# Hybrid decoder layer on Trainium2: the sums of the down stages, of the FFN-up stages and of one operand, moved from GpSimd to VectorE

## Chip, cores, metric

The kernel runs on one core of one Trainium2 chip. The metric is the device time in microseconds of one execution; smaller is better. The times shown are the median of several runs. The profile is one execution recorded by the hardware profiler.

The engines are named in the profile as PE (TensorE, matmuls), PEld (TensorE's weight loads), DVE (VectorE), ACT (ScalarE), POOL (GpSimd) and SP (SyncE, which issues all the transfers here). Each takes its instructions in order.

## The reference, cut to what matters

One layer of a hybrid decoder. After a mixing part (a gated linear recurrence and a gated real recurrence side by side), which the change does not touch, comes a SwiGLU feed-forward network, and a final norm:

```python
# SEQ = 2048 tokens, D_MODEL = 1024, D_FF = 2816, all float32
    h = h + jnp.einsum('bse,ed->bsd', mixed, w_out[l])
    hn = rms_norm(h, ffn_norm_w[l])
    gate, up = jnp.split(jnp.einsum('bsd,df->bsf', hn, w_gate_up[l]), 2, axis=-1)
    h = h + jnp.einsum('bsf,fd->bsd', jax.nn.silu(gate) * up, w_down[l])
return rms_norm(h, final_norm_w)
```

## The kernel before, in words

The 2048 tokens are worked in two halves of 1024 (half 0 and half 1), and a half in two column blocks of 512 tokens. In time the order is: projections and recurrences of half 0, of half 1, FFN-up of half 0, the down stage of half 0, FFN-up of half 1, the down stage of half 1 with the final norm and the stores of the output.

Every float32 operand of a matmul is split in two (`split`): ScalarE rounds it to a high part, VectorE subtracts that from the original and gets the low part. A product is three matmuls: high by high, high by low, low by high. A matmul here has a 128x128 stationary and a 128x512 moving operand.

The FFN's matrix products go by a scheme of Strassen's kind (in Winograd's form): of two by two blocks, seven products `p1` to `p7` are formed from sums and differences of blocks, instead of eight, and the four result blocks are sums of products. So beside the splits there are sums ahead of the products (of weights and of activations) and after them.

- `acts` makes the activation operands of FFN-up, from tiles b11, b12, b21, b22 that are read back from DRAM into `xin` and other tiles. `two` forms the differences; one of them (b12) is on GpSimd.
- `ffn_up` runs over 11 pairs of 256 columns of the FFN width per half, and for each over m = 0 (gate) and m = 1 (up): a "quad" of seven products (L582, tiles `quad_a`, `quad_e`, `quad_f`, `quad_g` in PSUM). The next quad's weights (`Sums.make`, tiles `wgu_a` to `wgu_g`) are made one product at a time between the products of the present one. After each product come a copy or sums out of PSUM (`e1`, `e5`, `u2`, `u3`), SiLU, and the multiplication of gate and up.
- `store` writes the result of a pair to DRAM. For most pairs it first forms four sums of the result blocks (s1 to s4, in `xin` tiles named `as`), which are the activation operands of the down stage; for the last three pairs of half 0 it stores the blocks as they are.
- `down_quads` is the down stage: result blocks h00, h01, h10, h11 (`hd` tiles in SBUF, loaded with the residual) of four token tiles each. The pairs are worked in groups of four: (0..3), (4..7) in half 0 and (0..3), (4..7), (8..10) in half 1. Within a group the products come in the order p1, p2, p6, p5, p3, p7, p4 (`DORDER`; the tiles have letters: p1 a, p2 b, p6 f, p5 e, p3 c, p7 g, p4 d). A product has, for each of four token tiles, 3 matmuls for each pair of the group, at L834: 48 in a group of four, 36 in the group of three. p1 and p2 add up in the same PSUM bank, so do p5 and p3, and p7 and p4.
- `Group.load` fetches the four down-weight blocks (`wdax`, `wdbx`, `wday`, `wdby`), `Group.fetch` the stored activations into raw tiles (`ra_`), and `Group.make` forms the operands of one product, a quarter (one pair of the group) at a time: the splits of the weights (`wd_`) and of the activations (`aop_`), and for p1 and p6 the differences of the weight blocks, of which three are on GpSimd and one (`wdt`) on VectorE. The loop calls it after each token tile's matmuls, for the next product.
- After each token tile of a product its PSUM bank is read. Two partial sums (`e1` = p1 + p6 and `e5` = p5 + p7, in SBUF) are formed with ScalarE copies and VectorE adds, and GpSimd adds them to the result blocks; p2, p3 and p4 are added to them by VectorE.
- In half 0 the last three pairs go through `down_plain` (L721 to L723), an ordinary product, while `acts` runs for half 1 beside it.
- `finish` does the final norm of a token tile and stores it; it is called inside the last group of half 1.

`tt_(out, a, b, op, e)` is an elementwise operation of two operands, on VectorE where no engine is named. Tiles come from pools with a set number of slots: `xin` 4, `late` 5, `block` (128 x 4 x 512) 14, `wslot` 9, `rawt` 3, `page` 16, and 8 banks of PSUM. A tile waits until a slot is free. The order of the instructions on each engine is written by a planner at compile time, which takes them from the program by priority and by times that it assumes (`schedule_with_timeline_sim=True`); it may place work of a later product ahead of an earlier one's. SP issues its transfers in that order too.

Of the kernel before, what the change touches and what calls it, by code (L numbers as in the profile page):

```python
# [13 lines left out]
P = 128  # L14
# [21 lines left out]
def hybrid_layer(ctx: ExitStack, tc: tile.TileContext, x, x_t, norm_w, cols, w_in, gate_w, w_out, w_gu, w_down, out):  # L36
# [453 lines left out]
    def acts(src, nm, direct):  # L490
        ops = {}
        held = []

        def put(name, k, p):
            split([ops[name][s][:, k, :] for s in range(2)], p)

        pages = {}

        def load(k):
            if k == 0:  # L500
                for name in ("p1", "p5", "p6", "p7", "p2") + (("p3", "p4") if direct else ()):
                    ops[name] = [block(f"act_{LET[name]}{s}_{nm}") for s in range(2)]
            b11, b12 = (xin(f"{t}{k}_{nm}") for t in ("b11_", "b12_"))
            b21, b22 = ((late if direct else page)(f"{t}{k}_{nm}") for t in ("b21_", "b22_"))
            for p, n, c in ((b11, 0, 0), (b12, 0, 1), (b22, 1, 1), (b21, 1, 0)):
                nc.sync.dma_start(out=p, in_=src[n][k, :, c * CW : (c + 1) * CW])
            pages[k] = b11, b12, b21, b22

        def one(k):
            b11, b12, b21, b22 = pages[k]  # L510
            put("p1", k, b11)
            tt_(b11, b12, b11, SUB_)
            put("p5", k, b11)

        def two(k):
            b11, b12, b21, b22 = pages[k]
            tt_(b11, b22, b11, SUB_)
            tt_(b12, b22, b12, SUB_, nc.gpsimd)
            put("p2", k, b21)
            put("p6", k, b11)  # L520
            tt_(b21, b21, b11, SUB_)
            put("p7", k, b12)
            if direct:
                put("p3", k, b22)
                put("p4", k, b21)
            held.append((b22, b21))

        def rest(i):
            name = ("p3", "p4")[i]
            ops[name] = [block(f"act_{LET[name]}{s}_{nm}") for s in range(2)]  # L530
            for k in range(4):
                put(name, k, held[k][i])

        steps = [lambda: load(0)]
        for k in range(4):
            steps.append(lambda k=k: (one(k), load(k + 1) if k < 3 else None))
            steps.append(lambda k=k: two(k))
        return ops, steps, [] if direct else [lambda: rest(0), lambda: rest(1)]
# [63 lines left out]
    def ffn_up(half, bops, between=()):  # L602
        between = list(between)
        q0 = half * 2 * NPAIR
        for q in range(q0, q0 + 2 * NPAIR):
# [7 lines left out]
            for i, name in enumerate(ORDER):  # L613
                if q == q0 and i not in s.done:
                    s.make(i)
                product(dst[name], s.op.pop(name), bops[name], i < 4)
                if name == "p1":
                    e1 = page("e1" + nm)
                    nc.scalar.copy(out=e1, in_=b1)
                elif name == "p5":  # L620
                    e5 = page("e5" + nm)
                    nc.scalar.copy(out=e5, in_=b3)
                elif name == "p6":
                    u2 = page("u2" + nm)
                    tt_(u2, e1, b2, ADD)
                elif name == "p7":
                    u3 = page("u3" + nm)
                    tt_(u3, u2, b4, ADD)
                    tt_(e5, u3, e5, ADD, nc.gpsimd)
                    if m == 0:  # L630
                        nc.scalar.activation(out=e5, in_=e5, func=AF.Silu)
                        sg22 = e5
                    else:
                        tt_(e5, e5, sg22, MUL, nc.gpsimd)
                        a22 = e5
                elif name == "p2":
                    if m == 0:
                        sg11 = page("sg11" + nm)
                        nc.scalar.activation(out=sg11, in_=b1, func=AF.Silu)
                    else:  # L640
                        tt_(sg11, sg11, b1, MUL)
                        a11 = sg11
                elif name == "p3":
                    tt_(e1, u2, b3, ADD)
                    if m == 0:
                        nc.scalar.activation(out=e1, in_=e1, func=AF.Silu)
                        sg12 = e1
                    else:
                        tt_(e1, e1, sg12, MUL)
                        a21 = e1  # L650
                else:
                    tt_(u2, u2, b4, ADD)
                    if m == 0:
                        nc.scalar.activation(out=u2, in_=u2, func=AF.Silu)
                        sg21 = u2
                    else:
                        tt_(u2, u2, sg21, MUL)
                        store(half, j, a11, u2, a21, a22)
                if nxt is not None and not end:
                    nxt.make(i)  # L660
                    nxt.done.add(i)
                if between:
                    between.pop(0)()
                if nn is not None and i in (0, 4) and quads[q + 2][0] == half:
                    nn.load(i // 4)
# [4 lines left out]
    def store(half, j, a11, a12, a21, a22):  # L670
# [2 lines left out]
                nc.sync.dma_start(out=a_d[half][2 * j + u][c], in_=p)  # L673
            return
        s1, s2, s3, s4 = (xin(f"as{i}_{half}_{j}") for i in range(4))
        g = nc.gpsimd
        tt_(s1, a21, a22, ADD, g)
        tt_(s2, s1, a11, SUB_, g)
        tt_(s3, a11, a21, SUB_, g)
        tt_(s4, a12, s2, SUB_, g)  # L680
        for name, p in (("p1", a11), ("p2", a12), ("p4", a22), ("p5", s1), ("p6", s2), ("p7", s3), ("p3", s4)):
            nc.sync.dma_start(out=ao_d[half][name][j], in_=p)

# [64 lines left out]
    class Group:  # L748
        def __init__(self, half, j0, n):
            self.half, self.j0, self.n, self.nm = half, j0, n, f"{half}_{j0}"  # L750
            self.a, self.w, self.b, self.raws = {}, {}, None, {}

        def load(self):
            wv = w_down[2 * self.j0 : 2 * (self.j0 + self.n)].rearrange("(g u) p (n w) -> u n p g w", u=2, n=2)
# [15 lines left out]
            self.raws[i] = rs  # L770


        def make(self, i, q):
            name = DORDER[i]
            if q >= self.n:
                return
            if q == 0:
                self.w[name] = [block(f"wd_{LET[name]}{s}_{self.nm}") for s in range(2)]
                self.a[name] = []
            if q % 2 == 0:  # L780
                self.a[name].append([wslot(f"aop_{LET[name]}{s}{q}_{self.nm}", (P, 2, CW)) for s in range(2)])
            b = {k: t[:, q, :] for k, t in self.b.items()}
            if name == "p6":
                if q == 0:
                    self.t2 = block(f"wdt_{self.nm}", F32)
                tt_(self.t2[:, q, :], b[1, 1], b[0, 0], SUB_)
            x = {"p1": b[0, 0], "p2": b[1, 0], "p5": b[0, 0], "p3": b[1, 1], "p7": b[0, 1], "p4": b[1, 0]}.get(name)
            if name == "p6":
                x = self.t2[:, q, :]
            split([self.w[name][s][:, q, :] for s in range(2)], x)  # L790
            split([self.a[name][q // 2][s][:, q % 2, :] for s in range(2)], self.raws[i][q // 2][:, q % 2, :])
            if name == "p1":
                tt_(b[0, 0], b[0, 1], b[0, 0], SUB_, nc.gpsimd)
            elif name == "p6":
                tt_(b[1, 0], b[1, 0], self.t2[:, q, :], SUB_, nc.gpsimd)
                tt_(b[0, 1], b[1, 1], b[0, 1], SUB_, nc.gpsimd)

    def down_quads(half, groups, hp, last):
        groups = [Group(half, j0, n) for j0, n in groups]
# [3 lines left out]
            if s < len(seq):  # L803
                seq[s][0].fetch(seq[s][1])

        def make(s, q):
            if s < len(seq):
                seq[s][0].make(seq[s][1], q)

        groups[0].load()  # L810
        fetch(0)
# [3 lines left out]
        for s, (gr, i) in enumerate(seq):  # L815
            name, nm = DORDER[i], gr.nm
            end = gr is groups[-1]
            if name == "p1":
                e1, e5 = {}, {}
            if name in ("p1", "p5"):  # L820
                ma = [bank(f"pda{name[1]}_{tt}_{nm}") for tt in range(TPC)]
            elif name in ("p6", "p7"):
# [4 lines left out]
            for tt in range(TPC):  # L827
# [8 lines left out]
                        )  # L836
                h00, h01 = hp[tt]
                h10, h11 = hp[TPC + tt]
                if name == "p1":
                    e1[tt] = late(f"e1_{tt}_{nm}")  # L840
                    nc.scalar.copy(out=e1[tt], in_=ps)
                elif name == "p2":
                    tt_(h00, h00, ps, ADD)
                elif name == "p6":
                    tt_(e1[tt], e1[tt], ps, ADD)
                    tt_(h01, h01, e1[tt], ADD, nc.gpsimd)
                elif name == "p5":
                    e5[tt] = xin(f"e5_{tt}_{nm}")
                    nc.scalar.copy(out=e5[tt], in_=ps)
                    tt_(h10, h10, e1[tt], ADD, nc.gpsimd)  # L850
                elif name == "p3":
                    tt_(h01, h01, ps, ADD)
                    tt_(h11, h11, e1[tt], ADD, nc.gpsimd)
                    if end and last:
                        finish(half, tt, hp[tt])
                elif name == "p7":
                    tt_(e5[tt], e5[tt], ps, ADD)
                    tt_(h11, h11, e5[tt], ADD, nc.gpsimd)
                else:
                    tt_(h10, h10, ps, ADD)  # L860
                    if end and last:
# [246 lines left out]
```

## Time and profile before

| | us |
|---|---|
| median of 3 runs (lowest, highest) | 2206.64 (2205.87, 2207.19) |
| the profiled execution | 2208.05 |
| its span, first to last instruction | 2206.3 |
| TensorE busy | 2121.9 (96%) |
| VectorE busy | 1508.5 (68%) |
| ScalarE busy | 1019.4 (46%) |
| GpSimd busy | 587.7 (27%) |
| FFN-up of half 0 and half 1 begin, about | 870, 1543 |
| down stage of half 0 and half 1 begin, about | 1295, 1962 |
| `down_plain` begins | 1467 |
| mean granted clock of TensorE | 0.985 |

A row of the page's groups gives line, engine, operation, written tile and read tiles, sizes and count, then busy time in all and mean ns of one, then how long the engine sat idle just before, and what ended most of that. A row of waits gives: engine and line, for whom, us in total, times, the longest. A row of the timeline gives: start, us, engine, line, operation, tiles, count of merged instructions, and in brackets the idle time before. A row of stretches gives: from:to, its length, then busy us and (instructions) of PE, PEld, DVE, ACT and POOL, then the granted clock, the busy share of the transfer engines, and GB/s.

A matmul's recorded time (some 390 ns) overlaps with the next one's, so the pitch, the time of a stretch over its matmuls, says more than the busy time.

### The profile page before, as it was taken

How to read it: one execution, taken by the hardware profiler on the slowest of the kernel's cores; microseconds unless marked ns; L12 is line 12 of the kernel's file. 1: busy time of each engine (PE TensorE's matmuls, PEld its weight loads, DVE VectorE, ACT ScalarE, POOL GpSimd, SP SyncE). 2: the span in 40 equal slices, each digit the busy share in tenths (PEclk: the TensorE clock that was granted, in tenths of full speed). 3: DMA queues.
4: the chain of work that ended last, by engine and by line, in shares of the span. 5: the costliest groups of instructions: out<-in, count | busy, mean ns of one | idle time of the engine just before them, and what ended most of it. 6: DMA issues, size and time to landing. Idle time of an engine off the chain costs nothing. (4 is left out here: it accounts for less than half of the span.)

```text
span 2206.3 us, 27183 instructions
## 1 busy us (share of the span) xinstructions
PE 2121.9 (96%) x9956; PEld 1744.7 (79%) x9956; DVE 1508.5 (68%) x2314; ACT 1019.4 (46%) x1757; POOL 587.7 (27%) x442
## 2 busy tenths in 40 slices
PE   8999899999999999999999998998999999998998
PEld 6778788887777887788888876887788888876876
DVE  5566664635677557866676579777767666679897
ACT  5467664535677545433333343444333333343443
POOL 1111110101111101223232146411323232356455
PEclk9999999999999999999999999999999999999999
DMA  6111105851110056423232264355423232355423
GB/s 220 58 39 39 39 20 169 285 167 30 38 39 29 20 181 230 150 98 106 91 125 91 96 227 164 115 160 169 134 91 124 91 124 91 105 209 196 153 86 139
DMA packets 137414, 261.33 MB, mean 118 GB/s; under 512 B 11072, under 2 KB 27456, under 8 KB 137280
## 3 DMA queue, kind: packets, MB, share of 16 engines
q1 hardware_dynamic: 137280, 259.59, 35.1%
q8 instruction: 78, 1.28, 0.2%
q14 instruction: 56, 0.46, 0.1%
HBM read 196.37 MB, written 63.18 MB: 118 GB/s over the span
## 5 line engine op out<-in xcount | busy, mean ns | idle before, releaser
L484 POOL TENSOR_TENSOR e<-u,e 128x512 f32<-128x512 f32 x44 | 77.3, 1757 | 525.3 <-ACT wgu_c L198 307.0
L484 POOL TENSOR_TENSOR hd<-hd,e 128x512 f32<-128x512 f32 x80 | 121.5, 1550 | 142.4 <-DVE e L484 142.3
L582 PE MATMUL quad_e<-act_e,wgu_e 128*128 128x512 f32 x528 | 129.2, 393 | 2.0 <-ACT wgu_e L198 1.9
L582 PE MATMUL quad_f<-act_f,wgu_f 128*128 128x512 f32 x528 | 127.1, 389 | 1.5 <-ACT wgu_f L198 1.5
L582 PE MATMUL quad_g<-act_d,wgu_d 128*128 128x512 f32 x528 | 127.6, 390 | 0.0
L582 PE MATMUL quad_a<-act_a,wgu_a 128*128 128x512 f32 x528 | 127.3, 389 | 0.0
L582 PE MATMUL quad_g<-act_g,wgu_g 128*128 128x512 f32 x528 | 127.1, 389 | 0.0
L582 PE MATMUL quad_a<-act_b,wgu_b 128*128 128x512 f32 x528 | 127.0, 389 | 0.0
L582 PE MATMUL quad_e<-act_c,wgu_c 128*128 128x512 f32 x528 | 126.8, 389 | 0.0
L582 PEld LDWEIGHTS quad_e<-act_e,wgu_e 128*128 128x128 f32 x528 | 100.1, 190 | 24.0 <-ACT wgu_e L198 2.6
L582 PEld LDWEIGHTS quad_f<-act_f,wgu_f 128*128 128x128 f32 x528 | 99.1, 188 | 22.4 <-ACT wgu_f L198 1.8
L582 PEld LDWEIGHTS quad_a<-act_a,wgu_a 128*128 128x128 f32 x528 | 98.9, 188 | 20.9 <-issue 0.4
L582 PEld LDWEIGHTS quad_a<-act_b,wgu_b 128*128 128x128 f32 x528 | 99.1, 188 | 20.6
L582 PEld LDWEIGHTS quad_e<-act_c,wgu_c 128*128 128x128 f32 x528 | 99.1, 188 | 20.6
L582 PEld LDWEIGHTS quad_g<-act_g,wgu_g 128*128 128x128 f32 x528 | 99.0, 188 | 20.6
L582 PEld LDWEIGHTS quad_g<-act_d,wgu_d 128*128 128x128 f32 x528 | 98.9, 188 | 20.4
L484 DVE TENSOR_TENSOR u<-u,quad_g 128x512 f32<-128x512 f32 x88 | 60.4, 686 | 79.3 <-PE quad_g L582 79.2
L226 PE MATMUL pb<-xn,wlo_in 128*128 128x512 f32 x256 | 102.7, 401 | 0.0
L225 PE MATMUL pb<-xn,whi_in 128*128 128x512 f32 x256 | 102.4, 400 | 0.0
L227 PE MATMUL pb<-xn,whi_in 128*128 128x512 f32 x256 | 101.8, 398 | 0.0
L155 DVE TENSOR_TENSOR wlo_in<-raw_in,whi_in 128x1024 fp32r<-128x1024 f32 x48 | 60.7, 1265 | 60.0 <-PE pv L238 40.6
L226 PE MATMUL pa<-xn,wlo_in 128*128 128x512 f32 x256 | 100.9, 394 | 0.0
(316 smaller groups left out, 5521.2 us busy)
## 6 DMA issues: line engine op xcount, KB each, us to landing
raw<-in_w_gu SPq DMA_DIRECT2D x88, 512.0 KB, 3.8
raw_in<-in_w_in SPq DMA_DIRECT2D x48, 512.0 KB, 3.5
ao_p<-as SPq DMA_DIRECT2D x76, 256.0 KB, 2.3
raw_o<-in_w_out SPq DMA_DIRECT2D x32, 512.0 KB, 4.7
x<-in_x SPq DMA_DIRECT2D x32, 256.0 KB, 5.3
xrh<-in_x SPq DMA_DIRECT2D x32, 256.0 KB, 3.9
h<-h SPq DMA_DIRECT2D x32, 256.0 KB, 3.7
hn<-hths SPq DMA_DIRECT2D x32, 256.0 KB, 4.5
```

The lines of the kernel that those rows point to most:

```text
L155: v.tensor_tensor(out=lo, in0=raw, in1=f(hi), op=ALU.subtract)
L225: nc.tensor.matmul(ps, lhsT=whi[:, ks], rhs=hi, start=(k == 0), stop=False)
L226: nc.tensor.matmul(ps, lhsT=wlo[:, ks], rhs=hi, start=False, stop=False)
L227: nc.tensor.matmul(ps, lhsT=whi[:, ks], rhs=lo, start=False, stop=(k == KT - 1))
L484: (e or v).tensor_tensor(out=out, in0=a, in1=b, op=op)
L582: nc.tensor.matmul(ps, lhsT=w[:, s, ks], rhs=x, start=first and k + n == 0, stop=k == 3 and n == 2, skip_group_check=not first)
```

## The change

- In `acts`, `ffn_up` and `store`, every sum that GpSimd did goes to VectorE.
- In the down stage GpSimd does no sums any more. p5 and p7 are added to h11 straight from PSUM, each by VectorE. p1 + p6 is added up over all the groups in one tile `u2` per token tile (four `xin` tiles, held through the whole down stage; ScalarE copies the first p1 into it), and only after p6 of the last group is it added to h01, h10 and h11.
- `Group.make` works in four parts of another cut: parts 0 and 1 split the weights, two pairs at a time (128x1024), parts 2 and 3 the activations, two pairs at a time. The differences of weight blocks are formed in one instruction over the whole group, on VectorE: `wdt` ahead of p6's part 0, and one after part 1 of each of p1, p6 and p5.

```diff
--- before.py
+++ after.py
@@ -515,7 +515,7 @@
         def two(k):
             b11, b12, b21, b22 = pages[k]
             tt_(b11, b22, b11, SUB_)
-            tt_(b12, b22, b12, SUB_, nc.gpsimd)
+            tt_(b12, b22, b12, SUB_)
             put("p2", k, b21)
             put("p6", k, b11)
             tt_(b21, b21, b11, SUB_)
@@ -626,12 +626,12 @@
                 elif name == "p7":
                     u3 = page("u3" + nm)
                     tt_(u3, u2, b4, ADD)
-                    tt_(e5, u3, e5, ADD, nc.gpsimd)
+                    tt_(e5, u3, e5, ADD)
                     if m == 0:
                         nc.scalar.activation(out=e5, in_=e5, func=AF.Silu)
                         sg22 = e5
                     else:
-                        tt_(e5, e5, sg22, MUL, nc.gpsimd)
+                        tt_(e5, e5, sg22, MUL)
                         a22 = e5
                 elif name == "p2":
                     if m == 0:
@@ -673,11 +673,10 @@
                 nc.sync.dma_start(out=a_d[half][2 * j + u][c], in_=p)
             return
         s1, s2, s3, s4 = (xin(f"as{i}_{half}_{j}") for i in range(4))
-        g = nc.gpsimd
-        tt_(s1, a21, a22, ADD, g)
-        tt_(s2, s1, a11, SUB_, g)
-        tt_(s3, a11, a21, SUB_, g)
-        tt_(s4, a12, s2, SUB_, g)
+        tt_(s1, a21, a22, ADD)
+        tt_(s2, s1, a11, SUB_)
+        tt_(s3, a11, a21, SUB_)
+        tt_(s4, a12, s2, SUB_)
         for name, p in (("p1", a11), ("p2", a12), ("p4", a22), ("p5", s1), ("p6", s2), ("p7", s3), ("p3", s4)):
             nc.sync.dma_start(out=ao_d[half][name][j], in_=p)
 
@@ -748,7 +747,7 @@
     class Group:
         def __init__(self, half, j0, n):
             self.half, self.j0, self.n, self.nm = half, j0, n, f"{half}_{j0}"
-            self.a, self.w, self.b, self.raws = {}, {}, None, {}
+            self.a, self.w, self.b, self.raws, self.t2 = {}, {}, None, {}, None
 
         def load(self):
             wv = w_down[2 * self.j0 : 2 * (self.j0 + self.n)].rearrange("(g u) p (n w) -> u n p g w", u=2, n=2)
@@ -770,30 +769,29 @@
             self.raws[i] = rs
 
 
-        def make(self, i, q):
-            name = DORDER[i]
-            if q >= self.n:
-                return
-            if q == 0:
+        def make(self, i, part):
+            name, n, b = DORDER[i], self.n, self.b
+            if part == 0:
                 self.w[name] = [block(f"wd_{LET[name]}{s}_{self.nm}") for s in range(2)]
-                self.a[name] = []
-            if q % 2 == 0:
-                self.a[name].append([wslot(f"aop_{LET[name]}{s}{q}_{self.nm}", (P, 2, CW)) for s in range(2)])
-            b = {k: t[:, q, :] for k, t in self.b.items()}
-            if name == "p6":
-                if q == 0:
+                self.a[name] = [[wslot(f"aop_{LET[name]}{s}{k}_{self.nm}", (P, 2, CW)) for s in range(2)] for k in range(0, n, 2)]
+                if name == "p6":
                     self.t2 = block(f"wdt_{self.nm}", F32)
-                tt_(self.t2[:, q, :], b[1, 1], b[0, 0], SUB_)
-            x = {"p1": b[0, 0], "p2": b[1, 0], "p5": b[0, 0], "p3": b[1, 1], "p7": b[0, 1], "p4": b[1, 0]}.get(name)
-            if name == "p6":
-                x = self.t2[:, q, :]
-            split([self.w[name][s][:, q, :] for s in range(2)], x)
-            split([self.a[name][q // 2][s][:, q % 2, :] for s in range(2)], self.raws[i][q // 2][:, q % 2, :])
-            if name == "p1":
-                tt_(b[0, 0], b[0, 1], b[0, 0], SUB_, nc.gpsimd)
-            elif name == "p6":
-                tt_(b[1, 0], b[1, 0], self.t2[:, q, :], SUB_, nc.gpsimd)
-                tt_(b[0, 1], b[1, 1], b[0, 1], SUB_, nc.gpsimd)
+                    tt_(self.t2[:, 0:n, :], b[1, 1][:, 0:n, :], b[0, 0][:, 0:n, :], SUB_)
+            k = 2 * (part % 2)
+            m = min(n, k + 2)
+            if part < 2:
+                x = {"p1": b[0, 0], "p2": b[1, 0], "p5": b[0, 0], "p3": b[1, 1], "p7": b[0, 1], "p4": b[1, 0]}.get(name, self.t2)
+                split([self.w[name][s][:, k:m, :] for s in range(2)], x[:, k:m, :])
+            else:
+                split([t[:, 0 : m - k, :] for t in self.a[name][k // 2]], self.raws[i][k // 2][:, 0 : m - k, :])
+            if part == 1:
+                d, x, y = {
+                    "p1": (b[0, 0], b[0, 1], b[0, 0]),
+                    "p6": (b[0, 1], b[1, 1], b[0, 1]),
+                    "p5": (b[1, 0], b[1, 0], self.t2),
+                }.get(name, (None, None, None))
+                if d is not None:
+                    tt_(d[:, 0:n, :], x[:, 0:n, :], y[:, 0:n, :], SUB_)
 
     def down_quads(half, groups, hp, last):
         groups = [Group(half, j0, n) for j0, n in groups]
@@ -803,9 +801,11 @@
             if s < len(seq):
                 seq[s][0].fetch(seq[s][1])
 
-        def make(s, q):
+        def make(s, part):
             if s < len(seq):
-                seq[s][0].make(seq[s][1], q)
+                seq[s][0].make(seq[s][1], part)
+
+        u2 = {}
 
         groups[0].load()
         fetch(0)
@@ -815,8 +815,6 @@
         for s, (gr, i) in enumerate(seq):
             name, nm = DORDER[i], gr.nm
             end = gr is groups[-1]
-            if name == "p1":
-                e1, e5 = {}, {}
             if name in ("p1", "p5"):
                 ma = [bank(f"pda{name[1]}_{tt}_{nm}") for tt in range(TPC)]
             elif name in ("p6", "p7"):
@@ -836,26 +834,28 @@
                         )
                 h00, h01 = hp[tt]
                 h10, h11 = hp[TPC + tt]
+
                 if name == "p1":
-                    e1[tt] = late(f"e1_{tt}_{nm}")
-                    nc.scalar.copy(out=e1[tt], in_=ps)
+                    if tt not in u2:
+                        u2[tt] = xin(f"u2_{tt}_{nm}")
+                        nc.scalar.copy(out=u2[tt], in_=ps)
+                    else:
+                        tt_(u2[tt], u2[tt], ps, ADD)
                 elif name == "p2":
                     tt_(h00, h00, ps, ADD)
                 elif name == "p6":
-                    tt_(e1[tt], e1[tt], ps, ADD)
-                    tt_(h01, h01, e1[tt], ADD, nc.gpsimd)
+                    tt_(u2[tt], u2[tt], ps, ADD)
+                    if end:
+                        for p in (h01, h10, h11):
+                            tt_(p, p, u2[tt], ADD)
                 elif name == "p5":
-                    e5[tt] = xin(f"e5_{tt}_{nm}")
-                    nc.scalar.copy(out=e5[tt], in_=ps)
-                    tt_(h10, h10, e1[tt], ADD, nc.gpsimd)
+                    tt_(h11, h11, ps, ADD)
                 elif name == "p3":
                     tt_(h01, h01, ps, ADD)
-                    tt_(h11, h11, e1[tt], ADD, nc.gpsimd)
                     if end and last:
                         finish(half, tt, hp[tt])
                 elif name == "p7":
-                    tt_(e5[tt], e5[tt], ps, ADD)
-                    tt_(h11, h11, e5[tt], ADD, nc.gpsimd)
+                    tt_(h11, h11, ps, ADD)
                 else:
                     tt_(h10, h10, ps, ADD)
                     if end and last:
```

## The prediction

> **What bounds the kernel now.** I read the page first (busy shares), then the waits of TensorE, then busy time by stretches, and last the instructions of VectorE and GpSimd inside the bad stretches.
>
> ```profile
> span 2206.3 us, 27183 instructions
> PE 2121.9 (96%) x9956; PEld 1744.7 (79%) x9956; DVE 1508.5 (68%) x2314; ACT 1019.4 (46%) x1757; POOL 587.7 (27%) x442
> L484 POOL TENSOR_TENSOR hd<-hd,e 128x512 f32<-128x512 f32 x80 | 121.5, 1550 | 142.4 <-DVE e L484 142.3
> ...
> PE pda L834 <- DVE aop_c L199: 15.7, 4, 7.4
> PE pdb L834 <- DVE wd_f L199: 6.2, 2, 3.2
> PE pd L721 <- ACT act_d L198: 3.6, 1, 3.6
> ```
>
> TensorE is busy nearly throughout, and its longest waits on VectorE lie in the down stages (L834). What they cost is seen in stretches. The first two rows hold the down products' matmuls alone (half 0, half 1), the others all engines: PE, PEld, DVE, ACT and POOL busy us, granted clock, DMA share, GB/s.
>
> ```profile
> 1298.06:1467.20 169.14, 157.80 (x671) 128.44 (x670) 0.96 0.46 151
> 1965.15:2196.40 231.25, 216.27 (x923) 174.98 (x922) 0.97 0.42 144
> ...
> 870.00:1294.00 424.00, 420.11 (x1864) 346.60 (x1865) 284.45 (x392) 162.75 (x290) 106.55 (x69) 1.00 0.33 114
> 1288.00:1346.30 58.30, 55.13 (x237) 45.16 (x236) 53.97 (x59) 29.76 (x57) 36.77 (x24) 0.97 0.75 269
> 1346.30:1369.30 23.00, 14.82 (x50) 10.72 (x49) 23.00 (x19) 5.99 (x11) 18.41 (x11) 0.78 0.31 93
> 1369.30:1467.20 97.90, 97.90 (x434) 81.06 (x433) 68.89 (x94) 36.85 (x65) 37.38 (x25) 1.00 0.39 121
> 1467.20:1541.00 73.80, 69.54 (x294) 56.37 (x293) 60.51 (x90) 38.35 (x73) 9.24 (x8) 0.95 0.53 175
> 1975.80:1994.20 18.40, 14.62 (x55) 10.94 (x53) 18.40 (x18) 9.85 (x20) 12.99 (x8) 0.91 0.36 125
> 2017.10:2038.90 21.80, 14.20 (x50) 10.39 (x50) 21.80 (x18) 5.99 (x11) 18.51 (x11) 0.77 0.30 97
> 2038.90:2127.10 88.20, 87.19 (x386) 71.91 (x384) 77.98 (x91) 37.44 (x68) 46.08 (x28) 1.00 0.39 128
> 2139.10:2196.40 57.30, 57.27 (x253) 47.11 (x251) 45.13 (x65) 25.89 (x57) 26.08 (x21) 1.00 0.34 115
> 2196.40:2206.30 9.90, 0.00 (x0) 0.00 (x0) 5.60 (x11) 2.56 (x8) 1.65 (x3) 0.66 0.57 213
> ```
>
> 1369.3 to 1467.2 holds nine products of 48 matmuls without a wait: 97.90 / 432 = 0.2266 us a matmul. At that pitch the down stages would need 671 x 0.2266 = 152.0 and 923 x 0.2266 = 209.2 us; they take 169.1 and 231.3. So 17.1 + 22.1 = 39.2 us are lost, nearly all in the first group of each half. The worst stretches are 1346.3 and 2017.1: there VectorE is busy for all of it (23.00 of 23.00, 21.80 of 21.80) and GpSimd for 80%. Part of a loss is an after-effect: the granted clock is 0.78 there, and the slowest matmul below takes twice the usual one.
>
> ```profile
> L834 PE MATMUL pda<-wd_c,aop_c x228: 387/389/797, 1346.3 to 2179.7; 128*128 128x512 f32 x114
> ...
> 1356.89 12.54 PE L834 MATMUL pda<-wd_c,aop_c 128*128 128x512 f32 x40 [7.42 <-DVE aop_c L199]
> ...
> 1319.13 2.48 DVE L199 TENSOR_TENSOR wd_c<-wdby,wd_c 128x512 fp32r<-128x512 f32 x4
> 1348.37 6.79 DVE L199 TENSOR_TENSOR wd_a<-wdax,wd_a 128x512 fp32r<-128x512 f32 x4
> 1355.09 3.43 DVE L199 TENSOR_TENSOR aop_c<-ra_c,aop_c 128x512 fp32r<-128x512 f32 x2
> 1367.60 1.87 DVE L484 TENSOR_TENSOR hd<-hd,pda 128x512 f32<-128x512 f32 x3
> ...
> 1351.23 6.74 POOL L484 TENSOR_TENSOR wdax<-wday,wdax 128x512 f32<-128x512 f32 x4
> 1504.55 1.21 DVE L199 TENSOR_TENSOR wlo_d<-raw_d,whi_d 128x1024 fp32r<-128x1024 f32 x1
> 2197.66 1.41 DVE L739 SCALAR_TENSOR_TENSOR hd<-hd,ss_f,wfin 128x512 f32<-128x512 f32 x2
> ```
>
> This is the cause. Four VectorE subtractions of 128x512 take 2.48 us, 0.60 each start to start. The same four take 6.79, 1.70 each, while GpSimd runs its own at 1.69 (6.74 / 4). TensorE waits 7.42 us for aop_c, which stands behind them. An add whose second operand is in PSUM keeps 0.60 (1.87 for three).
>
> **The change, part by part.** The sum is made against the profiled execution: 2208.05 us, 1.75 more than its span; the median shown, 2206.64, is 1.4 lower.
>
> VectorE's load in a down group of four. Before, its own instructions at 0.60: 56 splits, 20 adds and 4 subtractions (wdt), 48 us. GpSimd runs 16 adds of 1.55 and 12 subtractions of 1.69 beside it, 45 us, in which VectorE does 0.60/1.70 of its work: up to 29 us lost. Together 77 us, for 7 x 48 x 0.2266 = 76.1 us of TensorE: saturated. After: 28 splits of 128x1024 at 1.14 (1.21 less the 0.07 by which neighbours overlap), 32 us; 28 adds at 0.60, 17 us; four 128x2048 subtractions. These no row shows: the step from 0.60 to 1.14 for 512 more elements gives an estimate of 2.22, four narrow ones give 2.40; I take 2.2, so 9 us. Sum 58 of 76 us. For the VectorE page of the Trainium skill ("VectorE: DVE Perf Modes", section on the TRN2 errata) a 2048-element f32 tensor_tensor is 2.29 us; an estimate by it is 0.4 us more a group, and no run shows it yet. GpSimd's 45 us go.
>
> Last group of half 1 (three pairs): 14 splits of 1.14 and 14 of 0.60, 28 adds, 4 subtractions of 1.66, 12 adds of the sum u2, eight finishes of 1.35 (1.41 for the two of one): 24 + 17 + 7 + 7 + 11 = 66 us, for 57.1 of TensorE and the tail of 9.9. Tight, but before it held 50 and GpSimd's interference and lost almost nothing (57.30 us at 2139.1 for 252 matmuls, 57.1).
>
> What remains of the 39.2 us:
> (a) In p6 of the last group each token tile gets three more adds: 16 x 0.60 = 9.6, with p5's activations and its wide subtraction (2.3 + 2.2; 1.7 + 1.7 with three pairs) 14.1 us of VectorE against 10.9 of TensorE in half 0, 13.0 against 8.2 in half 1. From 0 (TensorE needs none of the adds, if p5's operands come first) to 3.2 + 4.8 = 8. I take 4.
> (b) u2 takes all four xin tiles for the whole down stage, where e5 took them late. In half 1 these last hold the sums of the last store, and p2, on p1's banks, waits for the copy into u2. ScalarE's queue holds its casts behind that copy.
>
> ```profile
> 1975.20 1.72 POOL L484 TENSOR_TENSOR as<-e,e 128x512 f32<-128x512 f32 x1
> 1987.05 1.74 POOL L484 TENSOR_TENSOR as<-u,as 128x512 f32<-128x512 f32 x1
> ...
> 1965.15 10.82 PE L834 MATMUL pda<-wd_a,aop_a 128*128 128x512 f32 x47
> ...
> ao_p<-as SPq DMA_DIRECT2D x7, 256.0 KB, 3.4
> ```
>
> The four sums end at 1988.8, and stores land 3.4 us after issue, while p1 ends at 1976.0: kept as late, this costs up to 16 us. On VectorE, each 0.60 after its last input, they can be out before. 0 to 16; I take 2, as three of the four need no input later than p3's product.
> (c) The planner's order is unknown: a wide instruction ahead of a needed one delays by 1.1 to 2.2 us, where it was 6.8. Later groups lost 0 (1369.3) and 88.20 - 384 x 0.2266 = 1.2 us: 0 to 10 over five groups, I take 4.
> Down stages: -39.2 + 10 = -29.
>
> Here one rule stands against the merge. "Perfetto Trace Analysis" of the Trainium skill (section on optimizing Scalar/DVE operations) advises breaking up instructions where an unsaturated engine causes bubbles elsewhere; by the rows, a half-width split is ready 0.54 us sooner, and with a wait in each of five groups the sum by it is 2.7 us less gain. No run shows this yet.
>
> Plain stage (L721): 73.80 - 294 x 0.2266 = 7.2 us lost.
>
> ```profile
> 1493.54 3.32 POOL L484 TENSOR_TENSOR b<-b,b 128x512 f32<-128x512 f32 x2 [13.70 <-DVE b L484]
> 1494.10 3.31 DVE L199 TENSOR_TENSOR act_e<-b,act_e 128x512 fp32r<-128x512 f32 x2
> 1503.57 0.76 PE L721 MATMUL pd<-whi_d,ad 128*128 128x512 f32 x1 [3.57 <-ACT act_d L198]
> ```
>
> Moving b12 to VectorE costs 0.60 a piece and frees 2.1 us of act_e's 3.3; on the path to act_d I take -2, between 0 and -7.
>
> FFN-up. 22 + 11 + up to 44 instructions a half go to VectorE, 77 x 0.60 = 46 us, and contention goes:
>
> ```profile
> L484 DVE TENSOR_TENSOR s<-raw,raw 128x512 f32<-128x512 f32 x44 | 45.4, 1032 | 42.3 <-DMA raw<-in_w_gu 42.3
> L484 DVE TENSOR_TENSOR s<-s,raw 128x512 f32<-128x512 f32 x44 | 46.0, 1046 | 1.3
> L484 DVE TENSOR_TENSOR u<-u,u 128x512 f32<-128x512 f32 x22 | 37.0, 1681 | 0.0
> L484 DVE TENSOR_TENSOR s<-raw,s 128x512 f32<-128x512 f32 x44 | 30.4, 691 | 1.6 <-DMA hn<-hths 0.4
> ```
>
> Against the undisturbed 0.69 that is 22 x (0.34 + 0.36) + 11 x 0.99 = 26 us back a half: 284 becomes about 305 of 424 us. TensorE does not wait there; what hides it is VectorE's 140 us of idle time, and if that cover went, the 20 us a half would be the price. I take 0 (-2 to +3). The tail (9.9 us with no matmul) keeps its chain: 0 (-1 to +1).
>
> Sum: -29 - 2 = -31: 2208.05 becomes 2177, and the median 2206.64 - 31 = 2175.6. All gone: -39.2 - 7.2 - 1 - 2, 2157. All ends bad: -39.2 + 34 + 4, about 2205.
>
> **The rivals.**
> Half the gain: VectorE still ends last at the first groups, or is saturated in the last ones; (a) to (c) then cost 20 to 30: 2186 to 2200, say 2191. For it: 66 of 67 us of load in the last group. Against it: 58 of 76 us elsewhere, and GpSimd's 45 us, which cost VectorE up to 29. "Perfetto Trace Analysis" of the Trainium skill, in the section already named, says that offloading to GpSimd may make sense where DVE is saturated, which speaks for this rival; no run shows it yet.
> No change: the first groups wait for transfers, which move no sooner, 2206. For it: DMA share 0.75 from 1288. Against it: 0.31 and 93 GB/s where TensorE stands still.
> Slower: activations late. Parts 0 and 1 now make weights, and the raw tiles come free only at parts 2 and 3, while the next fetch is still asked for at the second token tile, so SP stands there with the next loads behind it.
>
> ```profile
> 1365.30 5.76 SPq L768 DMA_DIRECT2D ra_a<-ao_p  x2
> ...
> ra_a<-ao_p SPq DMA_DIRECT2D x2, 512.0 KB, 3.6
> ```
>
> Now already the second of a pair is issued up to 5.8 us after the first. If it comes half a product (5.4 us) later and lands 3.6 after issue, it may miss the next product's start. Each of 35 products late by 0.9 us cancels the 31; by 2 us, 70 - 31 gives 2246. Against it: activation tiles come free only at a product's end, so the splits were no earlier before.
>
> **How the numbers follow.** Likeliest, most of the loss gone (2157 to 2186): 0.66. Half: 0.18. No change: 0.05. Slower: 0.11. Within 0.2% (4.4 us) counts as the same, about what a measurement here can tell. Half and likeliest are both faster, 0.84. The range 2160 to 2203 leaves out the slower case, no change and a little of the best end.
>
> **What would show it.** GpSimd without f32 128x512 sums in the down stages; wd and aop splits at 1.2 us for twice the width, none at 1.7 per 512; the stretches after p1 and in p3 of the first groups near 0.2266 us a matmul at clock 1.00; FFN-up unchanged in length. Wrong would be: waits of pda or pdb for aop or wd of over 3 us, u2's copy waiting for a store's DMA, casts waiting for ra tiles in steady groups.

## The result, and the profile after

The changed kernel takes 2168.0 us (median; 2166.54 to 2170.55), the kernel before 2206.26 in the same series: 0.9828 of it, 95% interval 0.9811 to 0.9845. That is 38 us less, inside the range given (2160 to 2203), 7.6 below the number 2175.6. Its profiled execution took 2167.16, with a span of 2165.5 where it was 2206.3.

The head of the page, after:

```profile
span 2165.5 us, 26664 instructions
PE 2108.4 (97%) x9956; PEld 1740.6 (80%) x9956; DVE 1483.9 (69%) x2395; ACT 993.8 (46%) x1599; POOL 131.4 (6%) x155
```

The longest of TensorE's waits for an aop or wd tile (total us, times, longest):

```profile
PE pdb L832 <- DVE aop_f L199: 4.4, 1, 4.4
```

GpSimd's busy time went from 588 to 131 us, and VectorE, which took over its sums, is busy 25 us less than before (1483.9 for 1508.5), with 81 instructions more (2395 for 2314). Of the waits for aop and wd tiles one is left.

The stretches after. First the down products' matmuls alone, up to p4's last (half 0, half 1), as the first two rows shown of before:

```profile
1295.42:1447.50 152.08, 152.08 (x671) 125.79 (x670) 1.00 0.49 165
1939.17:2156.10 216.93, 212.53 (x923) 175.07 (x922) 0.98 0.46 155
```

Then all engines (length, then PE, PEld, DVE, ACT and POOL busy with their counts, granted clock, DMA share, GB/s):

```profile
865.00:1292.50 427.50, 423.55 (x1871) 350.03 (x1870) 297.45 (x453) 161.48 (x278) 5.62 (x4) 0.99 0.35 118
1295.40:1447.50 152.10, 152.10 (x672) 125.98 (x671) 126.15 (x142) 60.09 (x68) 0.00 (x0) 1.00 0.49 165
1447.50:1514.00 66.50, 66.07 (x291) 54.19 (x290) 53.60 (x82) 34.55 (x66) 2.84 (x5) 1.00 0.55 182
1949.80:1965.70 15.90, 11.52 (x38) 8.90 (x37) 12.76 (x14) 2.15 (x3) 0.00 (x0) 0.79 0.91 319
2156.10:2165.50 9.40, 0.00 (x0) 0.00 (x0) 4.98 (x9) 2.16 (x8) 1.26 (x3) 0.72 0.49 185
```

Half 0's down stage takes 152.1 us where it took 169.1: nothing above the pitch is left of the 17.1 us lost. Half 1's takes 216.9 where it took 231.3; 923 x 0.2266 = 209.2, so 7.7 of the 22.1 remain. `down_plain` takes 66.5 where the stretch took 73.8. The tail is 9.4 for 9.9.

VectorE's instructions in half 1's down stage, in order of time, after (start, duration):

```profile
1935.08 1.22 DVE L199 TENSOR_TENSOR wd_b<-wdbx,wd_b 128x1024 fp32r<-128x1024 f32 x1
1941.35 2.29 DVE L484 TENSOR_TENSOR wdt<-wdby,wdax 128x2048 f32<-128x2048 f32 x1
1943.55 2.29 DVE L484 TENSOR_TENSOR wday<-wdby,wday 128x2048 f32<-128x2048 f32 x1
```

And the group of one product of FFN-up:

```profile
L484 DVE TENSOR_TENSOR u<-u,u 128x512 f32<-128x512 f32 x22 | 15.1, 686 | 0.0
```

A split of twice the width takes 1.22 us, where the narrow one took 1.70 beside GpSimd; a 128x2048 difference takes 2.29, and 2.20 from start to start. The product u<-u,u of FFN-up, 1.68 us before, takes 0.69.

The 7.7 us of half 1 are nearly all at one place: from 1949.80 to 1965.70, 38 matmuls, 8.6 us at the pitch, take 15.90. TensorE's rows there:

```profile
1939.17 10.82 PE L832 MATMUL pda<-wd_a,aop_a 128*128 128x512 f32 x47
1949.82 1.98 PE L832 MATMUL pdb<-wd_f,aop_f 128*128 128x512 f32 x8
1956.17 9.74 PE L832 MATMUL pdb<-wd_f,aop_f 128*128 128x512 f32 x29 [4.38 <-DVE aop_f L199]
1965.75 2.88 PE L832 MATMUL pda<-wd_b,aop_b 128*128 128x512 f32 x12
```

ScalarE's rows there, with what ended the wait before each:

```profile
1960.57 0.58 ACT L841 COPY u<-pda 128x512 f32<-128x512 f32 x1 [9.20 <-DMA ao_p<-as]
1970.85 1.20 ACT L841 COPY u<-pda 128x512 f32<-128x512 f32 x2 [3.43 <-DMA ao_p<-as]
```

The store's four sums on VectorE:

```profile
1951.42 0.69 DVE L484 TENSOR_TENSOR as<-e,e 128x512 f32<-128x512 f32 x1
...
1959.43 0.70 DVE L484 TENSOR_TENSOR as<-as,sg 128x512 f32<-128x512 f32 x1
1960.03 0.70 DVE L484 TENSOR_TENSOR as<-sg,e 128x512 f32<-128x512 f32 x1
1960.64 0.70 DVE L484 TENSOR_TENSOR as<-u,as 128x512 f32<-128x512 f32 x1
```

p1's bank is free for p2 only when ScalarE has copied it to u2, and u2 stands in xin tiles that the last store's sums (as) still hold: ScalarE waits 9.20 us for their transfer. Two things make the sums and their transfers late. In VectorE's order splits for p5, p6 and p3 stand between the first sum and the second, which starts 8 us after it; and the transfers land 9.5 us after issue (median of the four), where the row of before had 3.4, while the transfer engines are busy for 0.91 of this stretch. In TensorE's order p6 stands ahead of p2 there, and waits 4.38 us for its own activations; the granted clock of the whole stretch is 0.79.

### The profile page after: what moved, and what is told of

Same layout as the page of the kernel before. It is cut to its first block, busy times and chain, and to the rows that moved or that the text cites. A ratio compares the mean times of both kernels' runs of the same rounds, so it can differ in the third digit from the quotient of the medians.

```text
span 2165.5 us, 26664 instructions
## 1 busy us (share of the span) xinstructions
PE 2108.4 (97%) x9956; PEld 1740.6 (80%) x9956; DVE 1483.9 (69%) x2395; ACT 993.8 (46%) x1599; POOL 131.4 (6%) x155
## 4 chain that ended last, share of the span: by engine, by line
PE 78%; ACT 8%; DVE 8%; DMA 2%; issue 2%; POOL 1%; DVEq 0%; SPq 0%; ACTq 0%; POOLq 0%
PE quad_e L582 11%; PE quad_a L582 11%; PE quad_g L582 11%; PE pda L832 9%; PE pdb L832 6%; PE quad_f L582 6%; PE poh L237 2%; PE poh L239 2%; PE poh L238 2%; PE pb L226 1%; PE pb L227 1%; PE pb L225 1%; DMA b<-hn 1%; PE pa L225 1%; PE pa L226 1%
## 5 line engine op out<-in xcount | busy, mean ns | idle before, releaser
L238 PE MATMUL poh<-wlo_o,mx 128*128 128x512 f32 x256 | 99.5, 392 | 1.2 <-DVE wlo_o L155 1.2
L225 PE MATMUL pa<-xn,whi_in 128*128 128x512 f32 x256 | 100.5, 393 | 0.0
```

Of the source, the lines that this page charges most:

```text
L225: nc.tensor.matmul(ps, lhsT=whi[:, ks], rhs=hi, start=(k == 0), stop=False)
L238: nc.tensor.matmul(ps, lhsT=hi, rhs=wlo[:, ks], start=False, stop=False)
```

## The experiments

The theory was the prediction's: GpSimd's sums slow VectorE's two-input instructions, and where VectorE's load then passes TensorE's time, TensorE waits. Rivals: the wide instructions and the carried sum made the gain; the moves in FFN-up made it; TensorE had been waiting for GpSimd's results. Each time is a median beside the kernel before on the same chip; the ratio to it, with its interval, is what is compared.

**Only the engine of the down sums.** The kernel before, and:

```diff
-            tt_(h01, h01, e1[tt], ADD, nc.gpsimd)    # and h10, h11 with e1, h11 with e5
+            tt_(h01, h01, e1[tt], ADD)
-            tt_(b[0, 0], b[0, 1], b[0, 0], SUB_, nc.gpsimd)    # and the two of p6
+            tt_(b[0, 0], b[0, 1], b[0, 0], SUB_)
```

> The kernel before, with only one thing changed: the seven kinds of down-stage sums that GpSimd did (three differences of weight blocks, four adds into h) go to VectorE; no wider instructions, no carried u2, FFN-up and the other operands as before. Theory (GpSimd's two-input sums slow VectorE's two-input sums from 0.60 to 1.70 us per 128x512): VectorE's load in a group of four is 76 x 0.60 + 28 x 0.60 = 62 to 65 us of 76, the 39 us lost in the down stages fall to under 12, time 2170 to 2185. Rival (the gain is of the wider instructions and of the carried sum): the down stages still lose over 25 us, time 2192 or more.

2167.66 us, 0.9825 (0.9808 to 0.9841): as fast as the whole change, and faster than the theory said. Half 1's down products in it:

```profile
1945.60:2154.90 209.30, 209.30 (x923) 173.06 (x922) 1.00 0.47 160
```

No loss at all, and half 0's take 152.09 us (1294.94 to 1447.03), the pitch too. The rival falls: this needs no wide instruction and no carried sum.

**Only the other sums.** The kernel before, with the changes of `acts`, `ffn_up` and `store` alone (their four edits in the diff).

> The kernel before, with only the sums of FFN-up, of the store and of b12 moved to VectorE; down stages as before. Theory: FFN-up had no loss to give back; the plain stage gains up to its 7 us and the start of FFN-up up to 3; the down stages still lose 35 to 42 us: time 2196 to 2204. Rival (the changed kernel's gain comes largely from VectorE being ahead after FFN-up): below 2190.

2194.36 us, 0.9944 (0.9929 to 0.9958): 12 us, between the two expectations. The down stages lose less than they were to:

```profile
1298.00:1464.50 166.50, 156.09 (x671) 125.82 (x671) 0.98 0.45 154
1955.40:2182.50 227.10, 216.21 (x923) 174.87 (x922) 0.98 0.43 146
```

By the pitch 14.5 and 17.9 us, where 35 to 42 together were expected and 39.2 were lost before. Before, GpSimd did the four `as` sums and the last quad's sums inside half 1's first group; that their move to VectorE is the cause was not tried by itself. The plain stage gave back its 7 us here too (65.9 us from its first matmul to FFN-up's):

**Only b12.** The kernel before, and `tt_(b12, b22, b12, SUB_)` without GpSimd.

> The kernel before with only the difference b12 on VectorE. Theory (the plain stage's loss came through GpSimd's b12 and the tiles it held): the plain stage loses under 2 us instead of 7, time 2198 to 2202. Rival (that gain came from VectorE being ahead through the moves in FFN-up): 2204 to 2208.

2201.46 us, 0.9977 (0.9968 to 0.9987), as the theory said. In its trace the plain stage runs from the first row to the last:

```profile
1461.01 0.39 PE L721 MATMUL pd<-whi_d,ad 128*128 128x512 f32 x1
...
1526.88 0.39 PE L723 MATMUL pd<-whi_d,ad 128*128 128x512 f32 x1
```

65.9 us where it was 72.7 (1467.2 to 1539.9). One instruction per step on another engine gives nearly the whole of that term. The time of the traced execution (2196.59, the lowest of ten) says less than the stage: there FFN-up of half 0 began at 863.0, and in the three traces with the same code up to there (up_sums_dve, all_sums_dve, reads_two) at 867.5 to 868.1.

**All sums, nothing else.** The two edits above together, on the kernel before.

> The kernel before, with all its GpSimd sums on VectorE (down stages, FFN-up, store, b12) and nothing else changed: narrow instructions, e1 and e5 as before. Theory (the move of engine is the whole gain, and the new cut with u2 costs its 7.8 us): 2153 to 2162. Rival (wide instructions and the carried sum give a part of the gain): 2166 or more.

2158.98 us, 0.9780 (0.9762 to 0.9799), which is better than the changed kernel (0.9828; the intervals do not meet). Both down stages run at the pitch:

```profile
1296.82:1448.90 152.08, 152.08 (x671) 125.79 (x670) 1.00 0.50 168
1939.88:2149.10 209.22, 209.22 (x923) 173.05 (x922) 1.00 0.48 161
```

So the new cut of `make` and u2 brought nothing here, and lost 7.7 us of what the move had won in half 1.

**u2 elsewhere.** The changed kernel, and:

```diff
-                        u2[tt] = xin(f"u2_{tt}_{nm}")
+                        u2[tt] = (late if half else xin)(f"u2_{tt}_{nm}")
```

> The changed kernel, with u2 of half 1 in tiles of the pool late instead of xin, which the last store's four sums hold. Theory (the 7.8 us that half 1's down stage still loses come from u2's copy waiting for those stores, so that the planner puts p6 ahead of p2): p2 follows p1, no wait for aop_f, 2158 to 2163. Rival (the loss is of VectorE's backlog at the group's start): 2166 to 2171.

2160.12 us, 0.9787 (0.9770 to 0.9805). Half 1:

```profile
1940.61:2149.80 209.19, 209.19 (x923) 173.05 (x922) 1.00 0.48 160
```

TensorE's rows at the place where the changed kernel lost them:

```profile
1940.61 10.82 PE L832 MATMUL pda<-wd_a,aop_a 128*128 128x512 f32 x47
1951.27 11.04 PE L832 MATMUL pda<-wd_b,aop_b 128*128 128x512 f32 x48
1962.14 11.04 PE L832 MATMUL pdb<-wd_f,aop_f 128*128 128x512 f32 x48
```

p2 follows p1 and the 7.7 us are gone. That the tiles of the store held u2 back is shown; the chosen slot, not VectorE's backlog, cost it: in this run too VectorE is busy for all of the 27 us from 1935 to 1962.

**Narrow pieces.** The changed kernel, with each split and difference in pieces of 128x512 (a loop over q around them).

> The changed kernel, with every split and every difference of weight blocks cut back into pieces of 128x512. Theory (VectorE has room: 62 of 76 us in a group of four): TensorE waits no longer than now, 2164 to 2172. By the Trainium skill's advice to break up instructions, operands are ready half a microsecond sooner: 2164 to 2167. Rival (the wide instructions carry the gain): 2175 or more.

2166.12 us, 0.9812 (0.9796 to 0.9828): not to be told from the changed kernel. The advice of "Perfetto Trace Analysis" in the Trainium skill (section on optimizing Scalar/DVE operations) to break up instructions would have given 2.7 us by the prediction's estimate, less than these intervals resolve. One trace has the wait for aop_f at 3.2 instead of 4.4 us.

**GpSimd reads for nothing.** The changed kernel, with `nc.gpsimd.tensor_tensor(out=carry[:, 0], in0=d, in1=d, op=ADD)` per token tile and product, d an idle tile touched by `nc.scalar.copy(out=d[:, 0, 0:4], in_=ps[:, 0:4])`.

> The changed kernel, with one added GpSimd sum of 128x512 per token tile and product in the down stages (28 a group), of a tile that nothing uses into a tile that nothing uses, released by a small ScalarE copy out of the product's bank; no other work depends on it. It computes nothing that the output needs. Theory (shared reading): while it runs VectorE's two-input SBUF instructions slow down to GpSimd's pace (128x1024 from 1.2 to over 2.5 us), the down stages lose 20 to 45 us again: 2188 to 2215. Rival (the old loss came from waiting for GpSimd's results, or from the planner's order): no dependence, so 2164 to 2174.

2195.87 us, 0.9952 (0.9934 to 0.9969): as the theory said, but not for its reason alone. Its trace shows TensorE waiting for the small copies, which wait for GpSimd:

```profile
PE pda L839 <- ACT sct L814: 5.9, 7, 2.1
PE pdb L839 <- ACT sct L814: 4.5, 4, 2.4
PE pd L720 <- ACT sct L814: 2.5, 3, 1.5
```

That is a coupling that the experiment made itself, 13 us of its 28, so it decides nothing.

**GpSimd writes for nothing.** The same copies, with three `nc.gpsimd.memset(d, 0.0)` in place of the sum.

> As the run with the added GpSimd sums, but the added work is three memsets of 128x512 (0.5 us each at the kernel's start), which write and read nothing. Theory (it is the reading of two inputs that meets VectorE's): VectorE's instructions keep 1.2 us per 128x1024, time 2164 to 2174. Rival (any busy GpSimd, or the small ScalarE copies, cost it): like the run with the sums, 2188 or more.

2169.28 us, 0.9828 (0.9809 to 0.9848): no effect. GpSimd is busy 81 us of half 0's 152, as the row of the stretch shows (POOL before the clock):

```profile
1298.00:1450.10 152.10, 152.10 (x672) 125.98 (x671) 125.49 (x143) 66.09 (x122) 81.03 (x160) 1.00 0.49 165
```

VectorE's splits keep their 1.22 (the group; total us, mean ns):

```profile
L199 DVE TENSOR_TENSOR aop_e<-ra_e,aop_e 128x1024 fp32r<-128x1024 f32 x4 | 4.9, 1222 | 0.6 <-PE pda L840 0.4
```

A GpSimd that is busy with memsets costs VectorE nothing; it is not its being busy as such.

**Reads again, released by GpSimd itself.** The sum as before, after `nc.gpsimd.tensor_copy(out=d[:, 0, 0:4], in_=h[:, 0:4])` of a result tile.

> The changed kernel with the added GpSimd sums once more, now released by a small GpSimd copy of four columns of the result tile that VectorE has just written, so that no PSUM bank and no ScalarE instruction waits for them (in the last group's p3 and p4 there are none). It computes nothing that the output needs. Theory (shared reading slows VectorE by itself): two-input splits of 128x1024 again at 1.5 to 1.9 us, 2180 to 2200, with TensorE waiting for aop and wd tiles. Rival (the 28 us of the first such run came from the ScalarE copies that TensorE waited for): 2166 to 2174.

2175.77 us, 0.9851 (0.9829 to 0.9873): between both expectations. Half 0 as one stretch:

```profile
1298.30:1450.50 152.20, 152.20 (x672) 125.93 (x672) 144.89 (x140) 57.66 (x65) 122.39 (x106) 1.00 0.49 163
```

And two of VectorE's groups there, an add from PSUM and a split with both inputs in SBUF:

```profile
L484 DVE TENSOR_TENSOR hd<-hd,pda 128x512 f32<-128x512 f32 x24 | 15.5, 675 | 0.5 <-PE pda L842 0.5
L199 DVE TENSOR_TENSOR wd_e<-wdax,wd_e 128x1024 fp32r<-128x1024 f32 x4 | 7.3, 1846 | 0.0
```

VectorE does slow down: this split takes 1846 ns for 1222 (the other 128x1024 splits 1.21 to 1.89 us), the add from PSUM keeps its time (675, and 685 in the changed kernel). But TensorE loses nothing in half 0: VectorE is busy 144.9 us, up from 126.2, and still under 152. What the run loses lies elsewhere: 3 us in the plain stage (69.5 for 66.2), 1.5 in half 1, 1 in the tail, and the rest ahead of the down stages. The theory needed its second half: interference costs time only from the point where VectorE is full. Two runs were to pass that point.

**Past the point.** The all-sums kernel (narrow instructions, no u2), with one added sum of two different tiles per token tile and product (`in0=d, in1=carry[:, 1]`), released in the same way.

> The kernel before with all sums on VectorE, and beside it one added GpSimd sum per token tile and product in the down stages, of two different tiles that nothing else uses, released by a small GpSimd copy of a tile just written. It computes nothing that the output needs. Theory (the loss begins where VectorE's load with the interference passes TensorE's time): without the added sums VectorE is busy 130 of half 0's 152 us; at the 0.65 us or so that each of the old sums cost it, 56 of them make 166, so half 0 loses 10 us or more and the time is 2175 to 2210. Rival (interference does not cost TensorE time unless a product waits for GpSimd's own result): 2157 to 2166.

2234.79 us, 1.0123 (1.0106 to 1.0140): slower than before, and beyond the expectation. Half 0:

```profile
1296.20:1466.10 169.90, 158.52 (x672) 127.83 (x671) 163.97 (x205) 64.14 (x117) 133.17 (x106) 0.96 0.47 150
```

The added sums, as a group:

```profile
L819 POOL TENSOR_TENSOR carry<-sct,carry 128x512 f32<-128x512 f32 x54 | 82.7, 1531 | 4.2
```

And half 0 of the all-sums kernel, without them:

```profile
1296.80:1448.90 152.10, 152.10 (x672) 125.98 (x671) 130.38 (x213) 66.07 (x121) 0.00 (x0) 1.00 0.50 168
```

VectorE goes from 130.4 us for 213 instructions to 164.0 for 205, so at the old rate those 205 would take 125.5: (163.97 - 125.5) / 54 = 0.71 us for each sum on GpSimd, its small copy included. The kernel before gives nearly the same: from 1298.06 to 1467.20 VectorE is busy 135.84 us with 161 instructions, 98.5 at the rate of all-sums, beside 55 sums on GpSimd, 0.68 for each. TensorE loses 17.8 us here, as much as before the change (17.1). No wait of VectorE, TensorE or ScalarE in the down stages is for the added sums in this trace, so the loss needs no result of GpSimd's. Half 1 lost more than forecast, 46.6 us (1966.15 to 2222.00), and VectorE was busy for 252.3 of these 255.9.

**Two per tile.** The changed kernel with two added sums of one tile with itself, released by GpSimd.

> The changed kernel with two added GpSimd sums (of one tile with itself) per token tile and product, where the last such run had one and its half 0 lost nothing (VectorE busy 145 of 152 us, against 126). Theory: the second adds another 19 us, 164 of 152: half 0 loses 8 us or more, the whole 2183 to 2215. Rival: as with one, 2170 to 2178.

2272.93 us, 1.0302 (1.0284 to 1.0320), far beyond the expectation. Here VectorE does wait for the small copies (31.8 us for u, 21.8 for h), so its size says little beyond the direction.

**Down sums back on GpSimd.** The changed kernel, with the differences (all but wdt) and u2's adds on GpSimd.

> The changed kernel with the differences of the weight blocks (all but wdt, in pieces of 128x512) and the adds of u2 into h on GpSimd again; the wide splits and the carried u2 stay. Theory: GpSimd has 20 us of sums a group where it had 45, VectorE 58 - 7 us and 13 of interference, under TensorE's 76: little is lost but for latency of GpSimd's own results, 2165 to 2180. Rival (what hurt was the wait for GpSimd's results): 2185 or more.

2177.07 us, 0.9864 (0.9846 to 0.9882), as expected: with fewer sums than before GpSimd costs 8 us by the two ratios, and TensorE's longest wait there is for aop_f (7.7 us).

## Why the prediction was right

*The cause.* Right, and shown: the engine of the sums alone gives the whole gain in the down stages (39.2 us were lost, and next to 0 in the run with only their engine changed). Its size was too large. The interference was put at up to 29 us for 45 us of GpSimd in a group, 0.65 of VectorE for each us; measured in the kernel before is 0.68 us for each sum, 37 us for the 86 of GpSimd in half 0, or 0.43. So the load of 77 us for a group of 76.1, "saturated", was too high as well: VectorE is busy 135.84 us in half 0, 68 for a group. The prediction's own rows show it: the second group has VectorE at 68.89 of 97.90 us and no loss. What was saturated is the first group of each half, where 23.00 of 23.00 and 21.80 of 21.80 stand, and there the loss was; the argument holds for these stretches, not for the average group.

*The residue of 10.* It came to 7.7, but out of other parts. (a), the extra adds of p6, was 4 and is 0: half 0 has no loss. (c), the planner's order, was 4 and is 0. (b), u2 in xin, was 2 and is the whole 7.7: it was placed and bounded (0 to 16) but undersized, because the prediction took it that three of the four sums would be out early and that a store lands in 3.4 us. The trace has the four `as` sums from 1951.42 to 1961.34, and the stores take 9.5. Two of the signs named for being wrong did appear here, and nowhere else in the trace: a wait for an aop tile of over 3 us (4.38), and u2's copy waiting for a store. The third, casts waiting for ra tiles, appears as well (5.01 us in half 1's last group), and TensorE lost nothing by it there.

*Plain stage.* The mechanism was right, the size off: -2 forecast, -7 measured, the end of its range. The working counted the two instructions that it showed, not the xin tiles that late b12 kept from the next loads; that this is the way is argued from the code and not tried.

*FFN-up, tail.* FFN-up of half 1 keeps its length (1540.1 to 1962.2, 422.1 us before; 1513.6 to 1936.2, 422.6 after). Half 0's down stage begins 2.6 us earlier, which the forecast didn't have: its FFN-up begins 4.8 us earlier (865.12 for 869.93) and takes 2.2 longer. That start scatters by as much: the eight traces with the changed kernel's code up to there have it from 865.1 to 870.9, and the run with only the down sums moved, which changes nothing ahead of it, has it at 865.4 where the kernel before had 869.9. The tail gives 0.5.

*Sum.* -39.2 + 7.7 - 7 - 3 makes -41 for the profiled executions, -31 forecast. Of the 10 between them the plain stage has 5, the residue 2, and the rest is mostly the earlier start, which was luck. A 128x2048 difference, taken as 2.2, is 2.20 from start to start. The page "VectorE: DVE Perf Modes" of the Trainium skill (section on the TRN2 errata) gives 2.29 for one alone, and the trace agrees (2.29).

*The rivals.* Half the gain: its mechanism did occur, in (b), at a smaller price. No change, transfers: no; none of TensorE's waits after is for a transfer. Slower, late raw tiles: the pairs of fetches do stand some 9 us apart in places, but no product misses its start by it. For half the gain the prediction cited a rule of "Perfetto Trace Analysis" in the Trainium skill (section on optimizing Scalar/DVE operations), that offloading may make sense where DVE is saturated. The same paragraph goes on that between DVE and GpSimd it might not help, and the runs here bear out that second half: a two-input sum moved off costs VectorE 0.68 to 0.71 us, and done by VectorE 0.60.

## What to carry to other kernels

Before work is handed to GpSimd, compare what it costs VectorE in slowed instructions with what it would cost there: for two-input sums in SBUF the first was somewhat the larger here (0.7 for 0.60 us), so the offload was for nothing. Interference shows in time only from where the loaded engine is full; look at stretches where it is busy 100%, not at its average of 68%. Even such a stretch costs nothing while the operands made ahead last (27 us of it in the run with u2 elsewhere). When a partial sum is made to live longer, look at who holds its tile's slot just before.

## What the runs showed of the hardware that was not expected

A GpSimd sum of one tile with itself takes as little as 1.04 us, of two different tiles 1.27 or more, and both slow VectorE's instructions with two inputs in SBUF (wd_e of 128x1024 from 1.22 to 1.85 us beside the first, aop_d of 128x512 from 0.68 to 1.42 beside the second), while memsets on GpSimd for 81 of 152 us leave them at 1.22.
